# RMSNorm with ReLU on one core: chunks of fifteen rows per partition instead of sixteen

## The chip, the core and the metric

The kernel runs on one core of a Trainium2 chip; the other cores are idle. The metric is the device time of one execution in microseconds (us). Six runs of the kernel before gave a median of 164.03 us (163.74 to 164.24).

## The reference

```python
batch, seq, dim = 16, 1024, 512          # x: float32
rms = np.sqrt(np.mean(x ** 2, axis=-1, keepdims=True) + eps)
x_norm = x / rms * gamma
return np.maximum(x_norm, 0).astype(np.float32)
```

That is 16,384 rows of 512 float32 numbers (2 KB a row). 33.55 MB are read and 33.55 MB are written; nothing is used twice except `gamma`, which is one row.

## The kernel before

The 16,384 rows are cut into eight chunks of 2,048 rows (4 MB each). In a chunk, each of the 128 partitions holds 16 rows that follow one another in DRAM, so the share of one partition is one run of 32 KB in DRAM and one run of 32 KB in SBUF. There are six chunk buffers, `slot0` to `slot5` (6 x 32 KB in each partition). A chunk is loaded into a slot, normalised in place and stored from it.

All chunk transfers are issued by SP (SyncE), one instruction per chunk: `load(i)` at line 59 and `store(i)` at line 62. They share one DMA queue (q1 in the profile), and each is spread over the core's 16 DMA engines. Four small loads of `gamma` (line 89) are issued by ACT (ScalarE) and go through another queue (q10).

The work of a chunk, `compute(i)`, is done in groups of G = 8 rows per partition:

- line 74 (ACT): eight squares, one per row, each with its sum collected into a column of `ss`. The squares themselves go to `junk` and are not used.
- line 76 (ACT): one square root over the eight sums.
- line 78 (DVE, VectorE): one multiplication of eight rows (128x4096) by `gamma`, in place.
- line 79 (DVE): one reciprocal of the eight roots.
- line 81 (DVE): eight times, one row multiplied by its reciprocal and clipped at zero, in place.

The order is written out by hand (the tile framework's scheduler is off). SP's instructions come in this order, where L is a load and S a store: L0 to L5, S0, S1, L6, S2, L7, S3, S4, S5, S6, S7. A store waits until DVE has finished its chunk. L6 goes into slot 0 and so waits until S0 has landed, and L7 waits in the same way for S1. SP holds back everything behind a waiting instruction. L4 and L5 also wait for semaphores that earlier small transfers used; in the trace they were issued at about 13.1 us.

```python
for i in range(min(nslots, nchunks)):
    compute(i)
nxt = nslots
for i in range(nchunks):
    store(i)
    if i >= 1 and nxt < nchunks:
        load(nxt); compute(nxt); nxt += 1
```

Of the kernel before, what the change touches and what calls it, by code (L numbers as in the profile page):

```python
# [1 line left out]

# [4 lines left out]

F32 = mybir.dt.float32
ALU = mybir.AluOpType
ACTF = mybir.ActivationFunctionType  # L10


@with_exitstack
def kernel(
    ctx: ExitStack,
    tc: tile.TileContext,
    x: bass.AP,
    gamma: bass.AP,
    eps: bass.AP,
    out: bass.AP,  # L20
):


    nc = tc.nc
    P = nc.NUM_PARTITIONS

    x2 = x.flatten_outer_dims()
    out2 = out.flatten_outer_dims()
    n, d = x2.shape
    rows = n // P  # L30
    inv_d = 1.0 / d
    xv = x2.rearrange("(c p k) d -> c p k d", p=P, k=16)
    ov = out2.rearrange("(c p k) d -> c p k d", p=P, k=16)

    K = 16
    G = 8
    nchunks = rows // K
    nslots = 6
    ngroups = K // G

    singles = ctx.enter_context(tc.tile_pool(name="singles", bufs=1))
    slots = ctx.enter_context(tc.tile_pool(name="slots", bufs=1))
    small = ctx.enter_context(tc.tile_pool(name="small", bufs=1))
    psum = ctx.enter_context(
        tc.tile_pool(name="psum", bufs=1, space=bass.MemoryType.PSUM))

    ctx.enter_context(tc.manual_schedule())

    gseed = singles.tile([P, d], F32, name="gseed")
    gamma_sb = singles.tile([P, d], F32, name="gamma_sb")  # L50
    eps_sb = singles.tile([P, 1], F32, name="eps_sb")
    junk = psum.tile([P, d], F32, name="junk")
    slot = [slots.tile([P, K, d], F32, name=f"slot{s}") for s in range(nslots)]
    ss = [small.tile([P, K], F32, name=f"ss{i}") for i in range(nchunks)]
    rms = [small.tile([P, K], F32, name=f"rms{i}") for i in range(nchunks)]
    rstd = [small.tile([P, K], F32, name=f"rstd{i}") for i in range(nchunks)]

    def load(i):
        nc.sync.dma_start(out=slot[i % nslots], in_=xv[i])

    def store(i):
        nc.sync.dma_start(out=ov[i], in_=slot[i % nslots])

    def gammaG():
        g = gamma_sb[:]
        return bass.AP(tensor=g.tensor, offset=g.offset,
                       ap=[g.ap[0], [0, G], g.ap[1]])

    def compute(i):
        xt = slot[i % nslots]  # L70
        for g in range(ngroups):
            a, b = g * G, (g + 1) * G
            for j in range(a, b):
                nc.scalar.activation(out=junk, in_=xt[:, j, :], func=ACTF.Square,  # L74
                                     accum_out=ss[i][:, j:j + 1])
            nc.scalar.activation(out=rms[i][:, a:b], in_=ss[i][:, a:b],  # L76
                                 func=ACTF.Sqrt, bias=eps_sb, scale=inv_d)
            nc.vector.tensor_mul(out=xt[:, a:b, :], in0=xt[:, a:b, :], in1=gammaG())  # L78
            nc.vector.reciprocal(out=rstd[i][:, a:b], in_=rms[i][:, a:b])  # L79
            for j in range(a, b):  # L80
                nc.vector.tensor_scalar(  # L81
                    out=xt[:, j, :], in0=xt[:, j, :],
                    scalar1=rstd[i][:, j:j + 1], scalar2=0.0,
                    op0=ALU.mult, op1=ALU.max)

    nc.vector.memset(gseed, 0.0)  # L86
    nc.vector.memset(eps_sb, eps)  # L87
    for q in range(0, P, 32):
        nc.scalar.dma_start(out=gseed[q:q + 1, :], in_=gamma[None, :])

    for i in range(min(nslots, nchunks)):
        load(i)
    nc.vector.stream_shuffle(gamma_sb, gseed, [0] * 32)  # L93
# [6 lines that stand above are left out]
            load(nxt)  # L100
            compute(nxt)
            nxt += 1


# [1 line left out]
_INS = ['x', 'gamma', 'eps']  # L106
_OUTS = [((16, 1024, 512), 'float32')]

_NUMBERS = {'eps': 9.999999747378752e-06}


# [26 lines left out]
```

## Time and profile before

| What | Value |
|---|---|
| Median of six runs | 164.03 us |
| The profiled execution's own time | 164.15 us |
| Its span, first to last instruction | 162.1 us |
| DVE busy | 124.6 us (77%) |
| ACT busy | 98.5 us (61%) |
| Moved by DMA | 67.14 MB, mean 414 GB/s over the span |
| Queue q1 (all chunk transfers) | 2304 packets, 96.9% of 16 engines |
| DMA issues by SP | 8 loads and 8 stores of 4096 KB |

The profiled execution lies 0.12 us above the median, and 2.05 us of its time lie outside the span. A row of a group table gives the line, engine and operation, the output and inputs, the shapes and the count; behind the bar stand the busy time, the mean of one instruction in ns, and the idle time just before these instructions. In the table by stretches of time, the DMA share is the mean of 16 engines, and a packet is counted whole where it starts, so that a short stretch can show a little over 1.00. A packet of q1 carries the 32 KB of one partition, and each transfer has one more small packet per engine that signals its end: 16 transfers x (128 + 16) = 2304.

### The profile page before, as it was taken

How to read it: one execution, taken by the hardware profiler on the slowest of the kernel's cores; microseconds unless marked ns; L12 is line 12 of the kernel's file. 1: busy time of each engine (PE TensorE's matmuls, PEld its weight loads, DVE VectorE, ACT ScalarE, POOL GpSimd, SP SyncE). 2: the span in 40 equal slices, each digit the busy share in tenths (PEclk: the TensorE clock that was granted, in tenths of full speed). 3: DMA queues.
4: the chain of work that ended last, by engine and by line, in shares of the span. 5: the costliest groups of instructions: out<-in, count | busy, mean ns of one | idle time of the engine just before them, and what ended most of it. 6: DMA issues, size and time to landing. Idle time of an engine off the chain costs nothing.

```text
span 162.1 us, 554 instructions
## 1 busy us (share of the span) xinstructions
DVE 124.6 (77%) x164; ACT 98.5 (61%) x274; POOL 0.2 (0%) x4
## 2 busy tenths in 40 slices
DVE  1001299999999999999999999999999999920000
ACT  2007999999999999999999199901998000000000
POOL 0000000000000000000000000000000000000000
DMA  7999999999999999999999999999999989999980
GB/s 243 405 413 477 404 428 469 398 420 477 396 445 447 396 388 396 469 428 404 471 412 420 469 404 420 477 396 412 485 388 445 461 388 469 437 396 469 428 388 24
DMA packets 2315, 67.14 MB, mean 414 GB/s; under 512 B 260, under 2 KB 260, under 8 KB 264
## 3 DMA queue, kind: packets, MB, share of 16 engines
q1 hardware_dynamic: 2304, 67.11, 96.9%
q14 instruction: 3, 0.02, 0.0%
q10 hardware_dynamic: 8, 0.01, 0.0%
HBM read 33.56 MB, written 33.55 MB: 414 GB/s over the span
## 4 chain that ended last, share of the span: by engine, by line
DVE 74%; DMA 8%; ACT 3%; issue 2%; DVEq 0%
DVE slot L78 43%; DVE slot L81 30%; DMA slot<-in_x_dram 8%; ACT junk L74 3%; DVE rstd L79 1%; DVEq L133 0%
## 5 line engine op out<-in xcount | busy, mean ns | idle before, releaser
L74 ACT ACTIVATE junk<-slot 128x512 f32<-128x512 f32 x128 | 76.8, 600 | 23.5 <-DMA slot<-in_x_dram 19.9
L78 DVE TENSOR_TENSOR slot<-slot,gamma_sb 128x4096 f32<-128x4096 f32 x16 | 70.7, 4417 | 4.2 <-ACT junk L74 4.2
L81 DVE TENSOR_SCALAR slot<-slot,rstd 128x512 f32<-128x512 f32 x128 | 52.1, 480 | 0.6
L74 ACT ACTIVATION_READ_ACCUMULATOR junk<-slot 128x1 f32 x128 | 23.9, 186 | 0.0
L93 DVE LOAD_MASK_SELECT gamma_sb<-gseed x1 | 0.0, 14 | 12.8 <-DMA gseed<-in_gamma_dram 12.8
L76 ACT ACTIVATE rms<-ss,eps_sb 128x8 f32<-128x8 f32 x16 | 4.8, 301 | 0.5
L79 DVE RECIPROCAL rstd<-rms 128x8 f32<-128x8 f32 x16 | 3.1, 194 | 0.0
L74 ACT ACT_TABLE_LOAD x1 | 1.3, 1283 | 2.9 <-issue 2.9
L76 ACT ACT_TABLE_LOAD x1 | 1.3, 1283 | 0.0
L86 DVE MEMSET gseed<- 128x512 f32 x1 | 0.5, 485 | 0.9 <-PEq L119 0.9
L93 DVE STREAM_SHUFFLE gamma_sb<-gseed 128x512 f32<-128x512 f32 x1 | 0.7, 723 | 0.0
L119 POOL MEMSET const-bfloat16-1.0<- 128x1 bf16 x1 | 0.1, 102 | 0.0
L119 POOL MEMSET const-uint8-127<- 128x1 uint8 x1 | 0.1, 102 | 0.0
L119 POOL MEMSET const-float32-0.0<- 128x1 f32 x1 | 0.1, 99 | 0.2 <-issue 0.2
L119 POOL MEMSET const-float32-1.0<- 128x1 f32 x1 | 0.1, 99 | 0.0
L87 DVE MEMSET eps_sb<- 128x1 f32 x1 | 0.1, 59 | 0.0
## 6 DMA issues: line engine op xcount, KB each, us to landing
slot<-in_x_dram SPq DMA_DIRECT2D x8, 4096.0 KB, 30.5
out_dram<-slot SPq DMA_DIRECT2D x8, 4096.0 KB, 35.4
gseed<-in_gamma_dram ACTq DMA_DIRECT2D x4, 2.0 KB
```

Source lines behind the costliest of these rows:

```text
L74: nc.scalar.activation(out=junk, in_=xt[:, j, :], func=ACTF.Square, accum_out=ss[i][:, j:j + 1])
L76: nc.scalar.activation(out=rms[i][:, a:b], in_=ss[i][:, a:b], func=ACTF.Sqrt, bias=eps_sb, scale=inv_d)
L78: nc.vector.tensor_mul(out=xt[:, a:b, :], in0=xt[:, a:b, :], in1=gammaG())
L79: nc.vector.reciprocal(out=rstd[i][:, a:b], in_=rms[i][:, a:b])
L81: nc.vector.tensor_scalar(out=xt[:, j, :], in0=xt[:, j, :], scalar1=rstd[i][:, j:j + 1], scalar2=0.0, op0=ALU.mult, op1=ALU.max)
L86: nc.vector.memset(gseed, 0.0)
L87: nc.vector.memset(eps_sb, eps)
L93: nc.vector.stream_shuffle(gamma_sb, gseed, [0] * 32)
L119: nc = _bacc.Bacc("TRN2", target_bir_lowering=False, num_devices=1)
```

## The change

The number of rows per partition in a chunk becomes a list, `ks = [15] * 8 + [8]`: eight chunks of 1,920 rows (3.75 MB) and a ninth of 1,024 rows (2 MB). The share of one partition is then a run of 30 KB in DRAM (16 KB in the ninth chunk). The address steps between partitions, and so between DMA engines, are multiples of 30 KB in place of multiples of 32 KB. `first` holds the first row of each chunk, counted per partition, and `rows_of` cuts the chunk's rows out of `x` or `out`. Groups of eight rows stay, so a chunk of fifteen is a group of eight and one of seven, and the multiplication by `gamma` takes 128x4096 and 128x3584.

SP's order becomes L0 to L5, S0, S1, L6, S2, L7, S3, L8, S4, S5, S6, S7, S8. L8 goes into slot 2 and waits until S2 has landed. There are 18 chunk transfers in place of 16, and 17 groups of rows in place of 16.

```diff
-    xv = x2.rearrange("(c p k) d -> c p k d", p=P, k=16)
-    ov = out2.rearrange("(c p k) d -> c p k d", p=P, k=16)
+    def rows_of(ap, i):
+        r0, k = first[i] * P, ks[i]
+        return ap[r0:r0 + k * P, :].rearrange("(p k) d -> p k d", p=P)
 
-    K = 16
+    ks = [15] * 8 + [8]
+    first = [sum(ks[:i]) for i in range(len(ks))]
+    assert sum(ks) == rows
+    K = max(ks)
     G = 8
-    nchunks = rows // K
+    nchunks = len(ks)
     nslots = 6
-    ngroups = K // G
...
-        nc.sync.dma_start(out=slot[i % nslots], in_=xv[i])
+        nc.sync.dma_start(out=slot[i % nslots][:, :ks[i], :], in_=rows_of(x2, i))
...
-        nc.sync.dma_start(out=ov[i], in_=slot[i % nslots])
+        nc.sync.dma_start(out=rows_of(out2, i), in_=slot[i % nslots][:, :ks[i], :])
...
-        for g in range(ngroups):
-            a, b = g * G, (g + 1) * G
+        for a in range(0, ks[i], G):
+            b = min(a + G, ks[i])
...
-            nc.vector.tensor_mul(out=xt[:, a:b, :], in0=xt[:, a:b, :], in1=gammaG())
+            nc.vector.tensor_mul(out=xt[:, a:b, :], in0=xt[:, a:b, :], in1=gammaG(b - a))
```

More of the change, by code (lines that the diff above doesn't have):

```diff
@@ L58, in load, with gammaG @@
     def load(i):
-        nc.sync.dma_start(out=slot[i % nslots], in_=xv[i])
+        nc.sync.dma_start(out=slot[i % nslots][:, :ks[i], :], in_=rows_of(x2, i))
     def store(i):
-        nc.sync.dma_start(out=ov[i], in_=slot[i % nslots])
-    def gammaG():
+        nc.sync.dma_start(out=rows_of(out2, i), in_=slot[i % nslots][:, :ks[i], :])
+    def gammaG(n):
         g = gamma_sb[:]
         return bass.AP(tensor=g.tensor, offset=g.offset,
-                       ap=[g.ap[0], [0, G], g.ap[1]])
+                       ap=[g.ap[0], [0, n], g.ap[1]])
     def compute(i):
         xt = slot[i % nslots]
-        for g in range(ngroups):
-            a, b = g * G, (g + 1) * G
+        for a in range(0, ks[i], G):
+            b = min(a + G, ks[i])
             for j in range(a, b):
```

## The prediction

> **What bounds the kernel now.** I read the page's activity in slices and its chain of waits first, because they seem to disagree.
>
> ```profile
> DVE  1001299999999999999999999999999999920000
> DMA  7999999999999999999999999999999989999980
> DVE 74%; DMA 8%; ACT 3%; issue 2%; DVEq 0%
> ```
>
> The chain names DVE for 74% of the span, but DVE goes quiet about 18 us before the end and DMA does not. The chain therefore follows DVE only up to the issue of the last store. To see which of the two sets the end I took SP's issues in order of time, SP's waits, and ACT's waits for loads 6 and 7.
>
> ```profile
> 73.15 0.34 SPq L59 DMA_DIRECT2D slot<-in_x_dram  x1
> 82.83 0.34 SPq L59 DMA_DIRECT2D slot<-in_x_dram  x1
> 143.07 0.33 SPq L62 DMA_DIRECT2D out_dram<-slot  x1
> ...
> SPq L133 <- DMA out_dram<-slot: 17.7, 1, 17.7
> ...
> 92.81 0.60 ACT L74 ACTIVATE junk<-slot 128x512 f32<-128x512 f32 x1 [3.60 <-DMA slot<-in_x_dram]
> 112.74 0.60 ACT L74 ACTIVATE junk<-slot 128x512 f32<-128x512 f32 x1 [7.37 <-DMA slot<-in_x_dram]
> ```
>
> These are landings on the slowest DMA engine: store 0 at 73.15 (load 6 is issued then), store 1 at 82.83, load 6 at 92.81, load 7 at 112.74, and the last store at 143.07 + 0.33 + 17.7 = 161.10. One transfer takes 82.83 - 73.15 = 9.68 us, and from load 7 to the end five transfers take 48.36 us, that is 5 x 9.67. So store 7, issued at 143.07, could not start before 161.10 - 9.68 = 151.4: it stood in the queue for about 8 us. The DMA queue is the bound from beginning to end, and DVE has 8 us to spare.
>
> How near the queue is to its own limit is in the table by stretches (columns: from and to, length, busy times, clock, DMA share, GB/s) and in the DMA rows of 62 to 156 us.
>
> ```profile
> 0.00:4.00 4.00, 0.49 (x2) 1.14 (x1) 0.20 (x4) 1.00 0.73 246
> 4.00:59.00 55.00, 40.42 (x53) 44.23 (x124) 0.00 (x0) 1.00 1.00 430
> 59.00:62.00 3.00, 3.00 (x1) 2.87 (x9) 0.00 (x0) 1.00 1.04 350
> 62.00:156.00 94.00, 80.66 (x110) 50.23 (x143) 0.00 (x0) 1.00 1.00 433
> 156.00:158.00 2.00, 0.00 (x0) 0.00 (x0) 0.00 (x0) 1.00 0.80 344
> 158.00:159.00 1.00, 0.00 (x0) 0.00 (x0) 0.00 (x0) 1.00 0.16 66
> 159.00:160.00 1.00, 0.00 (x0) 0.00 (x0) 0.00 (x0) 1.00 0.08 33
> ...
> q1 hardware_dynamic: 1386, 40.67, 100.3%
> ```
>
> The reader should see one rate, 430 GB/s while only loads run and 433 while loads and stores follow one another, and three places that fall short of it. The first is the start. The second is 59 to 62 us, where the loads give way to the first store: 3 x (1 - 350/433) = 0.6 us. The third is the end: after 158 us hardly more than two packets start (a share of 0.16 is 0.16 x 16 = 2.6 engine-us) and then one (0.08). Most engines have finished, and one or two come about 2 us late. From the DMA row, a 32 KB packet takes 100.3% x 94 us x 16 / (40.67 MB / 32 KB = 1241) = 1.216 us.
>
> The losses of the slowest engine can be read from the landings. The first load landed at 13.09 (the chain shows it for 0.73 + 12.36). From there to 73.15 six transfers took 60.06 us against 6 x 9.68 = 58.08: 1.98 lost. Store 1 to load 6 took 9.98: 0.30 lost. Load 6 to load 7, two transfers, took 19.93: 0.57 lost. After that nothing is lost. In all it is 2.85 us, and all of it lies where loads are still running.
>
> **The change part by part.** The same bytes move, so the stream term stays: 67.11 MB at 433 GB/s is 155.0 us before and after. What is left is small.
>
> *Packets.* Two more transfers mean 32 more completion packets and 256 more data packets, 18 more per engine. The rows show a small packet only once: the 2 KB of gamma in 6.0 to 6.2 us.
>
> ```profile
> q10 hardware_dynamic: 1, 0.00, 2.6%
> ```
>
> 2.6% of 0.2 us x 16 is 83 ns; at the big packet's rate (1216 ns for 32 KB) 2 KB are 76 ns. So a packet's fixed part is at most some 7 ns and at least nothing, and 18 of them cost 0 to 0.13 us. I take 0.1.
>
> *Two more transfers as such.* Landing follows landing by 9.68 us, which is 4.19 MB at 433 GB/s, so a queued transfer has no start cost of its own: 0. A rule speaks against the change here: the Trainium skill's page "SBUF — State Buffer", section "The DMA setup-cost knee", gives each transfer a fixed cost of roughly 2 us. By it the two transfers would add 4 us where nothing hides them, and the landings above disagree for a filled queue.
>
> *Does the queue stay filled?* Scaled by 15/16 a transfer takes 9.08 us, the ninth 4.84. Going through SP's order from load 0's landing (13.09 - 0.61 = 12.5) with the losses of before, store 0 lands at about 69.1 and lets load 6 go; store 1 lands at 78.2 and lets load 7 go; store 2 lands at about 96.6 and lets load 8 go. SP stands at load 8 meanwhile, with stores 4 to 8 behind it, but load 7 and store 3 (issued at about 78.5) are still ahead in the queue, 18 us of work. If that cover were gone, each us of SP's wait would be a us of idle queue. Cost: 0.
>
> *DVE and ACT.* DVE does a group of eight in 4.33 + 0.12 + 3.26 and some gaps = 7.74 us, and of seven in about 6.8. Eight chunks at 14.53 and the ninth at 7.74 are 124.0, as 8 x 15.48 = 123.8 was. It starts 0.6 us earlier, so store 8 is issued at about 142.7, while its turn in the queue comes at about 156: 13 us of cover. One more square root (301 ns) and reciprocal (194 ns) hide there. Load 8 lands at about 121, and DVE wants its chunk at 134.8. Cost: 0, and if the cover were gone, 0.2 us.
>
> *One more load among the stores.* This is the term that I do not get for nothing. Each load that ran between stores was followed by a loss on the slowest engine, 0.30 and 0.57 us, while stores alone lost none. Load 8 is a third such load. Its cost lies between 0 (store 0 to store 1 lost nothing) and 0.57; I take 0.4, near the mean of its two neighbours, because it stands in the same place, between two stores.
>
> *Address steps.* This is what the change is about, and the trace has no other step to compare with. The start, 59 to 62 us and the late engines are the only places where engines could hold each other up over addresses; 62 to 156 us runs at one rate for loads and stores. From above, the gain is at most the 2.85 us of losses. From the other side, a pattern that suits the memory less would show as a longer packet; 1% is 1.55 us. I take 0, since the rate is the same in all long stretches whatever mix of addresses was in flight.
>
> Here a rule bears on it: the same skill's page "DMA: Bandwidth & Descriptors", section "Latency and other measured facts", reports that row pitches of large powers of two slow a copy (207 GB/s each way at 512 KiB against 214 when padded). Our pitch is 32 KB, below all that it lists; if it held here, 3.3% of 155 us or 5 us would come back. The section "Where 436 GB/s comes from" puts the engines' ceiling at 435 GB/s, which would leave 0.7 us of the stream term to gain. The 433 GB/s row agrees with the second.
>
> *Sum.* 162.1 + 0.1 + 0.4 = 162.6 us of span, plus 2.05 around it = 164.65 for a profiled execution; less the 0.12 that it lies above the median, 164.5 us. A difference of 0.2% (0.33 us) is about what a measurement can tell from none.
>
> **The rivals.** *The address step does matter (faster).* For it: the change removes exactly the lockstep, and 2.85 us of losses have no named cause. Against it: 433 GB/s in all other stretches. It decides if the dip at 59 to 62 or the late engines at the end go. Half of the losses gone, less the 0.1, gives 162.7; all of them 161.3. Chance 0.28.
>
> *Nothing but the packets (same).* The late engines owe their lag to chance, not to the third load: 164.03 + 0.1 = 164.1. For it: loads alone, too, lost part of the 1.98 us. Chance 0.20.
>
> *The stream gets slower (slower).* 30 KB steps spread less evenly, or a 30 KB packet costs more than 15/16 of 1.216 = 1.140 us. At 1% this is 164.5 + 1.55 = 166. Against it: nothing in the trace shows a memory-side limit. Chance 0.12.
>
> **How the numbers follow.** My forecast, 164.5, has 0.40. Slower by over 0.2%: 0.40 + 0.12 = 0.52; same: 0.20; faster: 0.28. The range goes from the half-gain case, 162.7, to 165.6 (a stream slower by 0.7%); beyond these ends I leave about 0.1 on each side.
>
> **What would show it.** Right: 433 GB/s in the long middle stretch; the dip where loads end, now near 55 to 59 us; packets of 30 KB at 1.140 us; load 8 issued with two transfers ahead; and one or two engines late at the end by 2 to 3 us. Wrong: a middle rate that differs by 1% or more, an even end of all 16 engines, or an idle DMA slice around 96 us.

## The result, and the profile after

The changed kernel takes 164.54 us (median of 21 runs, 163.38 to 165.15) against 164.14 us for the kernel before on the same chips (42 runs, 163.72 to 164.70). The ratio is 1.0023, with a 95% interval of 1.0013 to 1.0034: slower by 0.4 us, which is little, but the interval leaves out no change. The profiled execution took 164.78 us with a span of 162.7 us.

SP's issues in order of time and its waits, and ACT's waits for loads 6 and 7, after:

```profile
69.04 0.34 SPq L64 DMA_DIRECT2D slot<-in_x_dram  x1
78.58 0.34 SPq L64 DMA_DIRECT2D slot<-in_x_dram  x1
96.82 0.34 SPq L64 DMA_DIRECT2D slot<-in_x_dram  x1
...
142.71 0.33 SPq L67 DMA_DIRECT2D out_dram<-slot  x1
...
SPq L138 <- DMA out_dram<-slot: 18.6, 3, 9.0
...
87.76 0.60 ACT L79 ACTIVATE junk<-slot 128x512 f32<-128x512 f32 x1 [3.73 <-DMA slot<-in_x_dram]
106.20 0.60 ACT L79 ACTIVATE junk<-slot 128x512 f32<-128x512 f32 x1 [6.63 <-DMA slot<-in_x_dram]
```

The order of events is the forecast one: loads 6, 7 and 8 go out at 69.04, 78.58 and 96.82 us, when stores 0, 1 and 2 have landed, and the last store is issued at 142.71. The end of the work is 142.71 + 0.33 + 18.6 = 161.64 us, 0.54 later than the 161.10 before. DVE still stands well ahead of the queue.

The rate, in the table by stretches, and q1's row of 60 to 82 us:

```profile
4.00:53.00 49.00, 35.08 (x45) 39.18 (x109) 0.00 (x0) 1.00 1.00 432
53.00:60.00 7.00, 6.96 (x11) 6.71 (x20) 0.00 (x0) 1.00 0.97 347
62.00:156.00 94.00, 80.30 (x106) 49.86 (x141) 0.00 (x0) 1.00 1.00 430
158.00:159.00 1.00, 0.00 (x0) 0.00 (x0) 0.00 (x0) 1.00 0.54 229
159.00:160.00 1.00, 0.00 (x0) 0.00 (x0) 0.00 (x0) 1.00 0.19 82
160.00:162.70 2.70, 0.00 (x0) 0.00 (x0) 0.00 (x0) 1.00 0.04 18
```

```profile
q1 hardware_dynamic: 345, 9.62, 101.4%
```

In 60 to 82 us, 9.62 MB are 313 packets of 30 KB, and 101.4% x 22 us x 16 / 313 = 1.140 us each, 15/16 of the 1.216 us of before. Loads alone run at 432 GB/s (430 before). The dip where loads give way to stores is there again, now within 53 to 60 us. It is not larger than before: from 50 to 82 us q1 moved 13.42 MB, and 13.27 MB before. Packets still start after 160 us, where before none did:

```profile
160.00:162.10 2.10, 0.00 (x0) 0.00 (x0) 0.00 (x0) 1.00 0.00 0
```

How late the slowest engine comes can be put into one number for every kernel here: *the loss after store 1*. Take the landing of store 1, add the time of all transfers still to come at the clean rate (9.68 us for 4 MB, so 9.08 for 30 KB per partition and 4.84 for 2 MB), and subtract that from the end of the last store. Before: 82.83 + 8 x 9.68 = 160.27 against 161.10, a loss of 0.83 us. After: 78.58 + 8 x 9.075 + 2 x 4.84 = 160.86 against 161.64, a loss of 0.78. One profile stands behind each such number, and two profiles of one kernel below differ by 0.46 us, so it is a guide to where time goes and not a measure of small effects.

### The profile page after: what moved, and what is told of

It is laid out like the page before. It is cut to its first block, busy times and chain, and to the rows that moved or that the text cites. A ratio compares the mean times of both kernels' runs of the same rounds, so it can differ in the third digit from the quotient of the medians.

```text
span 162.7 us, 566 instructions
## 1 busy us (share of the span) xinstructions
DVE 124.8 (77%) x166; ACT 98.8 (61%) x275; POOL 0.2 (0%) x4
## 4 chain that ended last, share of the span: by engine, by line
DVE 74%; DMA 7%; ACT 3%; issue 2%; DVEq 0%
DVE slot L83 43%; DVE slot L86 30%; DMA slot<-in_x_dram 7%; ACT junk L79 3%; DVE rstd L84 1%; DVEq L138 0%
## 5 line engine op out<-in xcount | busy, mean ns | idle before, releaser
L79 ACT ACTIVATE junk<-slot 128x512 f32<-128x512 f32 x128 | 76.8, 600 | 24.5 <-DMA slot<-in_x_dram 18.6
L83 DVE TENSOR_TENSOR slot<-slot,gamma_sb 128x4096 f32<-128x4096 f32 (+1 forms) x17 | 70.8, 4167 | 4.3 <-ACT junk L79 4.3
L81 ACT ACTIVATE rms<-ss,eps_sb 128x8 f32<-128x8 f32 (+1 forms) x17 | 5.1, 300 | 0.5
L84 DVE RECIPROCAL rstd<-rms 128x8 f32<-128x8 f32 (+1 forms) x17 | 3.3, 194 | 0.0
```

## The experiments

Theory A, the prediction's: the address step does nothing, and the third load among the stores costs the late engines time. Theory B: the step itself acts. Each kernel was timed beside the kernel before.

**Nine chunks with 32 KB steps.** The count of transfers and loads without the address step.

```diff
-    ks = [15] * 8 + [8]
+    ks = [16] * 7 + [8, 8]
```

> Seven chunks of 16 rows and two of 8: nine chunks, 18 transfers and a third load among the stores as after the change, but every address step stays a multiple of 32 KB (16 KB in the two small chunks). Theory A (the third load among the stores and the two more transfers cost the time, the address step nothing): as after the change, 0.3 to 0.6 us above before. Theory B (the 30 KB step itself costs time): 0 to 0.1 us above before.

164.43 us against 164.09; ratio 1.0020 (1.0007 to 1.0034). This is about the change's whole effect (1.0023), without its address step. The issues and the wait for the last stores:

```profile
82.60 0.34 SPq L64 DMA_DIRECT2D slot<-in_x_dram  x1
...
135.53 8.07 SPq L67 DMA_DIRECT2D out_dram<-slot  x2
...
SPq L138 <- DMA out_dram<-slot: 18.0, 3, 8.4
```

The loss after store 1: the rest is again 77.44 us, which makes 160.04; the end is 135.53 + 8.07 + 18.0 = 161.60, so 1.56 us were lost where the kernel before lost 0.83.

**Chunks of 17 and 15 in turn.** The address step without the counts.

```diff
-    ks = [15] * 8 + [8]
+    ks = [17, 15] * 4
...
-    slot = [slots.tile([P, K, d], F32, name=f"slot{s}") for s in range(nslots)]
+    slot = [slots.tile([P, ks[s], d], F32, name=f"slot{s}") for s in range(nslots)]
...
-        for a in range(0, ks[i], G):
-            b = min(a + G, ks[i])
+        for a, b in ((0, 8), (8, ks[i])):
```

> Eight chunks of 17 and 15 rows in turn: no step is a power of two (34 KB and 30 KB multiples), but there are 16 transfers and two loads among the stores as before. Theory A: within 0.2 us of before. Theory B: the step's effect alone, 0.3 us or more above before. If the step helps and the third load ate the gain: 0.3 us or more below before.

164.17 against 164.09; ratio 0.9999 (0.9986 to 1.0012). Steps of 34 and 30 KB, with 16 transfers and two loads among the stores, change nothing beyond some 0.2 us either way, the ends of the interval. Together with the run above this points to the counts and not to the step, but the two intervals still overlap a little (1.0007 to 1.0012); the kernels with their loads together, below, say the same.

**Five slots.** Three loads among the stores, transfers and steps as before.

```diff
-    nslots = 6
+    nslots = 5
```

> The kernel before with five slots in place of six: 16 transfers of 32 KB per partition, but three loads (5, 6, 7) among the stores. The queue stays filled by the same sums. Theory A: 0.3 to 0.5 us above before. Theory B and a lag by chance: within 0.2 us of before.

164.21 against 164.09; ratio 1.0008 (0.9991 to 1.0024). Inconclusive: the middle of the interval lies nearer to no change, and 0.3 us (1.0018) is not excluded. Its issues and its last wait show why the total says little:

```profile
72.33 0.34 SPq L59 DMA_DIRECT2D slot<-in_x_dram  x1
...
143.93 0.33 SPq L62 DMA_DIRECT2D out_dram<-slot  x1
...
SPq L133 <- DMA out_dram<-slot: 17.2, 1, 17.2
```

After store 1's landing, 72.33 + 9 x 9.68 = 159.45 against 161.46: a loss of 2.0 us with three loads among the stores. But store 1 landed 0.8 us earlier than one transfer less explains (82.83 - 9.68 = 73.15): the first change from loads to stores was cheaper here. The variant moves two things at once.

**Loads 6 and 7 together.** The kernel before, with one return from loads to stores after store 1 instead of two.

```diff
-        if i >= 1 and nxt < nchunks:
+        while i == 1 and nxt < nchunks:
```

> The kernel before with loads 6 and 7 issued one behind the other after store 1, so that the order has one return from loads to stores in the middle in place of two. Theory A, if the loss belongs to the change from loads to stores: 0.3 to 0.5 us below before. If the loss belongs to each load: within 0.1 us. If the lag of the late engines is chance: within 0.2 us.

> The kernel before with loads 6 and 7 one behind the other, run again beside the others. Theory A: again 0.3 to 0.5 us below before (0.9977 in the first run). If the first run was chance: within 0.2 us of before.

163.66 against 164.09, ratio 0.9977 (0.9963 to 0.9990); and again, 163.87 against 164.23, 0.9979 (0.9966 to 0.9993). The first run's issues (store 1 had landed when the second load went, at 73.60 + 10.01 - 0.34 = 83.27), ACT's wait for load 6, and SP's last wait:

```profile
73.60 10.01 SPq L59 DMA_DIRECT2D slot<-in_x_dram  x2
...
93.03 0.60 ACT L74 ACTIVATE junk<-slot 128x512 f32<-128x512 f32 x1 [3.75 <-DMA slot<-in_x_dram]
...
143.18 0.33 SPq L62 DMA_DIRECT2D out_dram<-slot  x1
...
SPq L133 <- DMA out_dram<-slot: 17.2, 1, 17.2
```

83.27 + 77.44 = 160.71, and the end is 143.18 + 0.33 + 17.2 = 160.71: nothing is lost after store 1. In the second run it was 0.46 us by the same sum, still less than the 0.83 of before. So the loss belongs less to a load than to a change between loads and stores.

The profiles also tell which change it is. Load 6 follows store 1 in all three kernels, and a clean transfer takes 9.68 us. With store 2 behind it, as before, load 6 landed 92.81 - 82.83 = 9.98 us after store 1; with load 7 behind it, 93.03 - 83.27 = 9.76 us, and 9.77 us in the second run. So going from a store to a load cost at most 0.1 us there. The larger losses of before, 0.30 and 0.57 us, came with loads that have a store behind them.

**The changed kernel with its three late loads together.** Steps of 30 KB and 18 transfers stay.

```diff
-        if i >= 1 and nxt < nchunks:
+        while i == 2 and nxt < nchunks:
```

> The kernel after the change with loads 6, 7 and 8 issued one behind the other after store 2: 30 KB steps and 18 transfers stay, the three returns from loads to stores in the middle become one. Theory A (each return from loads to stores costs the late engines 0.3 to 0.5 us): 0.6 to 0.9 us below the kernel after the change, so 163.6 to 163.9. If the 18 transfers as such cost the time: as after the change, 0.3 to 0.5 us above before.

163.67 against 164.23; ratio 0.9969 (0.9954 to 0.9985). Against the changed kernel's 1.0023 that is 0.0054 of 164.2 us, or 0.9 us less. 18 transfers as such cost nothing that shows. Nor does the 30 KB step: with their loads together, the kernel with 32 KB steps stood at 0.9977 and 0.9979 and this one at 0.9969. It is the fastest version here, level with the one above within their intervals.

```profile
69.17 18.48 SPq L64 DMA_DIRECT2D slot<-in_x_dram  x3
...
143.22 0.33 SPq L67 DMA_DIRECT2D out_dram<-slot  x1
...
SPq L138 <- DMA out_dram<-slot: 17.3, 3, 9.0
```

The first line merges the three loads; the second of them, by itself, was issued at 78.25, when store 1 had landed. So 78.25 + 82.28 = 160.53 against 160.85: 0.32 us lost, against 0.78 in the changed kernel.

**Four half loads.** Two more returns than before.

```diff
-    ks = [15] * 8 + [8]
+    ks = [16] * 6 + [8] * 4
```

> Six chunks of 16 rows and four of 8: 20 transfers and four loads among the stores, all steps multiples of 16 KB. Theory A: two more returns than before, 0.5 to 0.9 us above before (the nine-chunk run with one more showed 0.2%). If what costs is only the presence of a ninth transfer, not their number: 0.3 us above.

164.47 against 164.23; ratio 1.0020 (1.0009 to 1.0030). A miss for an additive cost: two more returns cost 0.3 us, no more than one more did. A fixed price for each return does not hold. The rival's 0.3 us for the presence of a ninth transfer fits this run, but not the run above, which has nine chunks and no such cost. The four late loads here are of 2 MB each, where before has two of 4 MB; whether the price of a return grows with the load ahead of it was not tried.

**Larger steps.** First the kernel before with 128 consecutive rows per partition, so that partitions lie 256 KB apart; then the changed kernel with 120 consecutive rows, 240 KB apart; and that one with its late loads together.

```diff
-    xv = x2.rearrange("(c p k) d -> c p k d", p=P, k=16)
-    ov = out2.rearrange("(c p k) d -> c p k d", p=P, k=16)
+    xv = x2.rearrange("(p c k) d -> c p k d", p=P, k=16)
+    ov = out2.rearrange("(p c k) d -> c p k d", p=P, k=16)
```

> The kernel before with 128 consecutive rows per partition over the whole kernel: each chunk's share of a partition is still one run of 32 KB, but the step from partition to partition is 256 KB in place of 32 KB, so the steps between DMA engines are larger powers of two. Theory A (addresses do not bear on this rate): within 0.3 us of before. Theory B (steps of powers of two hold the engines up): at least 1.5 us (1%) above before; by the Trainium skill's row for 512 KB steps up to 5 us.

```diff
-        r0, k = first[i] * P, ks[i]
-        return ap[r0:r0 + k * P, :].rearrange("(p k) d -> p k d", p=P)
+        if i < 8:
+            return ap[0:120 * P, :].rearrange("(p c k) d -> c p k d", p=P, k=15)[i]
+        return ap[120 * P:128 * P, :].rearrange("(p k) d -> p k d", p=P)
```

> The kernel after the change with 120 consecutive rows per partition for its first eight chunks: runs of 30 KB at steps of 240 KB, no power of two. Theory A: within 0.3 us of the kernel after the change (about 0.4 us above before). Theory B: clearly faster than the 256 KB variant, by 1.5 us or more.

> The 240 KB variant with loads 6, 7 and 8 one behind the other after store 2. It lay 1.2 us above the kernel after the change. If the address step acts only where loads give way to stores (Theory A widened): it loses 1.2 us or more, to 164.6 or below. If the step slows the stream itself: it loses no more than the 0.8 us of the fifteen-row kernel, and stays above 164.8.

Measured: 256 KB 164.62 against 164.27, ratio 1.0021 (1.0001 to 1.0041); 240 KB 165.75, ratio 1.0083 (1.0057 to 1.0109); 240 KB with the loads together 164.69 against 164.23, ratio 1.0032 (1.0018 to 1.0046). Theory B's forecast fails on both sides: the large power of two costs 0.2%, and the step that is no power of two is the slower of the two. Theory A's forecast for 240 KB fails as well: 1.2 us above the changed kernel, not 0.3. The issues and last wait of the 240 KB kernel, and its table by stretches:

```profile
78.71 0.34 SPq L65 DMA_DIRECT2D slot<-in_x_dram  x1
97.79 0.34 SPq L65 DMA_DIRECT2D slot<-in_x_dram  x1
...
143.07 0.33 SPq L68 DMA_DIRECT2D out_dram<-slot  x1
...
SPq L139 <- DMA out_dram<-slot: 19.7, 3, 9.0
```

```profile
4.00:53.00 49.00, 34.73 (x44) 39.27 (x109) 0.00 (x0) 1.00 1.00 430
60.00:82.00 22.00, 21.89 (x30) 21.12 (x61) 0.00 (x0) 1.00 1.01 437
```

In the stretch of loads it runs at 430 GB/s and in 60 to 82 us at 437, where the changed kernel ran at 432 and 437. No slower stream shows there, but the cost in question is 0.6%, about the difference between 430 and 432, so these rows do not exclude one. From store 1 to store 2, with load 6 between, it takes 19.08 us, where two transfers are 18.15. The loss after store 1 is 143.07 + 0.33 + 19.7 - (78.71 + 82.28) = 2.1 us; this profile is the slowest of only four executions (166.20 us against their median of 165.75). The same lines with the loads together (the first is the second of its three loads, issued when store 1 had landed):

```profile
79.14 0.34 SPq L65 DMA_DIRECT2D slot<-in_x_dram  x1
...
142.81 0.33 SPq L68 DMA_DIRECT2D out_dram<-slot  x1
...
SPq L139 <- DMA out_dram<-slot: 18.5, 3, 9.0
```

The end is 142.81 + 0.33 + 18.5 = 161.64, which leaves 161.64 - 79.14 - 82.28 = 0.2 us of the loss after store 1, and the medians give 1.1 us back. Neither forecast is met: 164.69 lies between the 164.6 or less of the widened theory and the 164.8 or more of its rival. What decides is the comparison with the 30 KB kernels. With the loads apart the 240 KB step cost 165.75 - 164.54 = 1.2 us, with the loads together 164.69 - 163.67 = 1.0 us (0.6% both times by the ratios). So putting the loads together helped both kernels about alike, and the cost of the 240 KB step stayed. It hardly depends on how often loads run among the stores. Where it falls is open: in the profiles with the loads together store 1 landed at 79.14 (240 KB) and 78.25 (30 KB), so there the difference arose before that, perhaps at the first change from loads to stores, which no run left out.

## Why the prediction was right

*The bound and the stream.* The forecast of 164.5 us stands beside 164.54. That they meet within 0.04 us is luck: the term for the third load could lie between 0 and 0.57 us, and the sum starts from a median of 164.03 for the kernel before, which stood at 164.14 in the runs beside the changed kernel. A rise of 0.5 us was forecast, and 0.4 us was measured. The queue stayed the bound and stayed filled, a 30 KB packet took 1.140 us, and the times at which SP issued loads 6, 7 and 8 and the last store came within 0.4 us of the sums (the prediction's own terms give 12.5 + 54.5 + 2.0 = 69.0 for the landing of store 0, where it wrote 69.1). The term for the long stretch, 0, holds: 433 GB/s before and 430 after in 62 to 156 us. What is missing stands in 62 to 110 us (433 and 429), where loads run among the stores, and not from 110 to 156 us (432 in both); but the kernel with its three loads together shows 433 and 429 in these two stretches, so rows of this kind scatter by a few GB/s.

*Packets and transfers.* 0.1 us for the packets and 0 for the two transfers as such cannot be told from nothing, and the kernel with 18 transfers and its loads together, 0.5 us faster than the kernel before, shows that they are small.

*The third load among the stores.* The sum gave it 0.4 us, the nine-chunk kernel measured 0.34 us for the same counts with 32 KB steps, and the kernels with their loads together took away 0.4 and 0.9 us. So the term was the right one, and its size fits within the intervals. Its form was wrong: it is not a price for each load. Two more loads, of half the size, cost as much as one more, and two loads behind one another cost less than two apart. Five slots, the plainest third load, measured 0.1 us, with an interval (0.15 below to 0.39 above) that neither confirms nor excludes 0.4.

*What the one profile of after does not show.* By the landings it lost 2.15 us up to store 0 (56.60 us from 12.44, against 6 x 9.075), 0.46 between stores 0 and 1, 0.10 up to load 6, nothing up to store 2, 0.30 up to load 7, and 161.64 - 106.20 - 55.06 = 0.38 from there to the end, where load 8 lies. The stretch with load 8 has its 0.38 us, but loads 6 and 7 lost less than before (0.40 against 0.87) and the part ahead of load 6 lost more. One execution against another can't carry a term of 0.4 us when runs of one kernel spread over 1.8 us; the timed comparisons carry it.

*The address step.* The rival that made the kernel faster falls: chunks of 17 and 15 give 0.9999. What was said for it, that 2.85 us of losses had no named cause, was true. The part of them that a run could move, about 0.4 us, followed the order of loads and stores; for the 1.98 us up to store 0 no run shows a cause. The row of the Trainium skill's page "DMA: Bandwidth & Descriptors" (section "Latency and other measured facts") on large powers of two lists steps from 512 KB up, with 207 GB/s there and 214 for a step of 4 MB padded by 4 KB; the prediction took its 3.3% from these two. Nothing like it showed here: at 256 KB, half the smallest step listed, the cost was 0.2%, and a step of 240 KB did worse.

## What to carry to other kernels

Before changing addresses for the sake of a transfer queue, divide its busy time by its packets in a long stretch: here loads and stores ran at one rate, and steps of 30 and 34 KB in place of 32 gave nothing. Then look where loads hand over to stores and how late the last engine is, since part of the remaining loss lay there; issuing the loads that must run between stores one behind the other gave 0.2 to 0.3%, more than the change under study moved. And undo the parts of a change one at a time: here a change of addresses also brought a third load among the stores, and the runs put its effect down to that.

## What the runs showed of the hardware

A step of 256 KB between partitions cost 0.2% against 32 KB (interval 0.01 to 0.41%), and one of 240 KB 0.6% against 30 KB, with the late loads apart and together. Why, and where in the run, was not settled. Loads that run among the stores cost time on the slowest engine when a store stands behind them: loads 6 and 7 lost 0.30 and 0.57 us before and 0.10 and 0.30 us after the change, while load 6 with a load behind it lost 0.1 us at most in both runs of loads 6 and 7 together. Why an engine falls behind there, whether late loads disturb stores that other engines have begun or the reverse, was not tried; a kernel that keeps them apart by waiting would leave the queue empty meanwhile. Nor is it settled why a second extra return costs nothing more.
